# Gate and up projections of a SwiGLU layer: from a seven-product scheme (2 x 2 x 2 blocks) to a twenty-product scheme (2 width blocks, 4 contraction parts, 3 token thirds)

## The chip, the core and the metric

The kernel runs on one core of a Trainium2 chip, as one program. Its engines work side by side, each through its own queue in order: TensorE (PE, with its weight loads, PEld), VectorE (DVE), ScalarE (ACT), GpSimd (POOL) and SyncE (SP, which here only issues loads). The metric is the device time of one execution in microseconds (us), the median over several. A profile of one execution gives every instruction's start and duration.

## The reference, cut to what matters

One encoder layer over two sequences (256 and 1024 tokens, 1280 in all, width 1024): a norm, an input projection, two kinds of attention, an output projection, a residual, then

```python
h2 = rmsnorm(x, ffn_norm_g)
x = x + (jax.nn.silu(h2 @ w_gate) * (h2 @ w_up)) @ w_down
```

and a final norm. `w_gate` and `w_up` are 1024 x 2816, `w_down` is 2816 x 1024, all in float32. The change lies in `h2 @ w_gate` and `h2 @ w_up`.

## The kernel before, in words

**A product in three passes.** Every float32 operand is split into a high part (rounded to the matmul's format, by a cast on ACT) and a low part (the rest, by a subtraction). `mm3` adds three matmuls into one PSUM tile: high x high (line 110), high x low (111), low x high (112). A weight operand is "cast on ACT, low half on POOL"; a token operand is "cast on ACT, low half on DVE".

**The stage in question (M, after its PSUM tile; 791 to 1340 us of the span).** The width of 2816 is taken in eleven pairs of 128 columns (`fp`). For each pair and each of the two matrices (i = 0 gate, i = 1 up; I call one matrix of one pair a unit) the product of weights (2 width blocks x 2 contraction halves) and tokens (2 contraction halves x 2 token halves) is made by a scheme of seven products (`SEQ`), each of a sum of weight blocks with a sum of token blocks, where eight would be needed plainly. The token sums `S[m]` are made once, in and before the first pair, and kept; the weight sums are made in every unit: `sum_A` adds on POOL, `split_A` makes the two halves in a ring `wc` of six tiles. `product` runs four contraction chunks of `mm3` for each half of 640 tokens, 320 columns a time (24 matmuls), and then its result is copied (ACT, line 1050) or added (DVE, line 1052) to the unit's output `C`. Some products continue the PSUM tile of another one (`CHAIN`), so that the earlier result is read from it first.

**After a pair.** `finish` takes silu of the gate blocks (ACT, 1067), multiplies (DVE, 1069) and makes the sums that the down projection's own seven-product scheme needs (DVE, 1080); the seven results go to DRAM as `act_d[1]` to `act_d[7]`, 320 KB each, issued from ACT's queue (from POOL's in the last pair).

**What stands before.** For each of ten blocks of 128 tokens, the output projection (`out_proj`), the residual and the second norm (`ffn_in`) with transposes; the transposed block is scaled into `R` (DVE and ACT), and its token sums are begun. For blocks 0 to 4, S1 and S2 are split at once; for blocks 5 to 9 the differences are made on POOL. **What stands after** is the down projection; its first four steps are loaded and split by `down_first` inside the last pair.

**The order of work.** SP's loads stand in the order of the code. The other four engines' instructions are ordered by a scheduler at build time, which may draw an instruction ahead or put it back; `tc.issue_after(x)` keeps what it encloses behind instruction x. On the chip each engine works through its queue strictly in the order so found.

```python
def operand(A, m, ...):           # one product's weight operand
    if m == 6: ...                # s1 = A21 + A22; s2 = s1 - A11; s4 = A12 - s2 (POOL)
    if m == 7:
        sum_A(A["21"], A["11"], A["21"])
    return split_A(A[...])        # cast on ACT, subtraction on POOL
```

## Time and profile before

| | us |
|---|---|
| median of three runs (1612.8 to 1613.93) | 1613.7 |
| span of the profiled execution, first to last instruction | 1610.3 |
| what lies around the span, by difference to the median | 3.4 |
| the ten token blocks (output projection, second norm) | about 690 to 791 |
| the M stage | 791 to 1340 |
| the down projection and the end | 1340 to 1610 |

The profiled execution's own time is its span of 1610.3 us. The page gives the busy time of every engine, then groups of equal instructions: their line, engine and operation, the tiles written and read, partitions x elements, their count, total busy time and the mean of one in ns, and the idle time of the engine before them with what ended it. A matmul's duration reaches from its issue to its modelled end and overlaps the next one; the rate is the distance of starts, that is a stretch's length over its number of matmuls.

### The profile page before, as it was taken

Reading aid. Unit: us, or ns where it says so; the run is one execution under the profiler, and the core shown is the slowest. Engines: PE = TensorE matmul, PEld = TensorE weight load, DVE = VectorE, ACT = ScalarE, POOL = GpSimd, SP = SyncE. Lnnn points to the kernel's source line nnn. Section 1 sums busy time; section 2 is a strip of 40 time slices with the busy share of each in tenths; the row PEclk is TensorE's granted clock in tenths of the full one; section 3 lists DMA queues with packets and bytes.
Section 4 is the critical chain, followed back from the end, with each engine's and each line's share of the span. In section 5 each row is a group of like instructions: output and inputs, shape, how many; then the busy total and the mean of one; then the engine's idle time right before and its main releaser. Section 6 shows DMA issues by size and latency. Waiting matters only on the chain.

```text
span 1610.3 us, 25767 instructions
## 1 busy us (share of the span) xinstructions
PE 1582.5 (98%) x9616; PEld 1443.1 (90%) x9616; DVE 893.3 (55%) x1501; ACT 717.2 (45%) x1492; POOL 666.1 (41%) x833
## 2 busy tenths in 40 slices
PE   8999999999999999999999999999999999999998
PEld 8998789998888888888899999999999998888886
DVE  5853045566677777443583444334444246886676
ACT  6533144465777777544453323233222332443334
POOL 4633235544211129224676665565666651010002
PEclk9999999999999999999999999999999999999999
DMA  8626022152100030234312232222232237843534
GB/s 294 202 70 160 19 53 63 37 209 62 32 20 26 24 119 20 80 118 144 125 67 65 89 110 97 71 87 89 97 110 76 70 128 269 296 140 96 157 103 155
DMA packets 121772, 171.09 MB, mean 106 GB/s; under 512 B 35376, under 2 KB 65840, under 8 KB 121648
## 3 DMA queue, kind: packets, MB, share of 16 engines
q1 hardware_dynamic: 78880, 120.30, 24.3%
q10 hardware_dynamic: 41952, 46.08, 8.2%
q0 software_dynamic: 816, 3.08, 0.5%
q8 instruction: 75, 1.23, 0.3%
q14 instruction: 49, 0.40, 0.1%
HBM read 118.96 MB, written 50.46 MB: 105 GB/s over the span
## 4 chain that ended last, share of the span: by engine, by line
PE 90%; POOL 3%; ACT 2%; DVE 2%; DMA 1%; issue 1%; SPq 0%; ACTq 0%; POOLq 0%; DVEq 0%
PE M L112 11%; PE M L110 10%; PE M L111 10%; PE d L111 5%; PE d L110 5%; PE d L112 5%; PE o L788 4%; PE tp L778 4%; PE na_o L512 3%; PE po L110 2%; PE pj L110 2%; PE pj L111 2%; PE pj L112 2%; PE po L111 2%; PE po L112 2%; PE S L110 2%
## 5 line engine op out<-in xcount | busy, mean ns | idle before, releaser
L111 PE MATMUL M<-S,wc 128*128 128x320 f32 x1056 | 323.8, 308 | 0.0
L110 PE MATMUL M<-S,wc 128*128 128x320 f32 x1056 | 321.3, 309 | 2.5 <-ACT S L962 1.2
L112 PE MATMUL M<-S,wc 128*128 128x320 f32 x1056 | 312.0, 309 | 2.4 <-POOL wc L970 2.4
L110 PEld LDWEIGHTS M<-S,wc 128*128 128x128 f32 x1056 | 197.3, 188 | 3.7 <-ACT S L962 1.5
L111 PEld LDWEIGHTS M<-S,wc 128*128 128x128 f32 x1056 | 198.2, 188 | 0.0
L112 PEld LDWEIGHTS M<-S,wc 128*128 128x128 f32 x1056 | 194.7, 188 | 3.0 <-POOL wc L970 3.0
L970 POOL TENSOR_TENSOR wc<-A,wc 128x512 fp32r<-128x512 f32 x86 | 121.1, 1409 | 81.6 <-ACT wc L969 81.5
L1052 DVE TENSOR_TENSOR z<-M,z 128x320 f32<-128x320 f32 x120 | 57.2, 487 | 129.6 <-PE M L112 109.1
L969 ACT CAST wc<-A 128x512 fp32r<-128x512 f32 x86 | 53.5, 622 | 158.4 <-PE M L111 148.8
L970 POOL TENSOR_TENSOR wc<-sum,wc 128x512 fp32r<-128x512 f32 x62 | 88.5, 1427 | 85.8 <-ACT wc L969 85.7
L1052 DVE TENSOR_TENSOR zB<-M,zB 128x320 f32<-128x320 f32 x100 | 47.6, 488 | 133.4 <-PE M L112 109.9
L111 PE MATMUL d<-S,S 128*128 128x512 f32 (+1 forms) x314 | 121.1, 386 | 0.0
L112 PE MATMUL d<-S,S 128*128 128x512 f32 (+1 forms) x314 | 120.7, 386 | 0.0
L110 PE MATMUL d<-S,S 128*128 128x512 f32 (+1 forms) x314 | 120.4, 387 | 0.0
L100 DVE TENSOR_TENSOR PT<-tp,PT 128x512 fp32r<-128x512 f32 (+1 forms) x144 | 93.2, 658 | 33.9 <-ACT PT L99 32.7
L969 ACT CAST wc<-sum 128x512 fp32r<-128x512 f32 x62 | 38.4, 619 | 144.0 <-PE M L111 99.6
L99 ACT CAST PT<-tp 128x512 fp32r<-128x512 f32 (+1 forms) x144 | 79.2, 567 | 33.5 <-PE tp L778 30.2
L770 DVE TENSOR_REDUCE mm<-S 128x1 f32<-128x1024 f32 (+1 forms) x80 | 85.0, 1062 | 13.5 <-PE S L112 11.9
L1099 ACT CAST S<-as 128x640 fp32r<-128x640 f32 x58 | 42.2, 728 | 105.7 <-issue 62.7
L772 ACT ACTIVATE ex<-S,mm 128x1024 f32<-128x1024 f32 (+1 forms) x80 | 79.7, 997 | 14.9 <-DVE mm L770 13.6
L801 POOL TENSOR_TENSOR ob<-ob 128x128 f32<-128x128 f32 x40 | 18.5, 461 | 160.8 <-ACT ob L798 157.3
L788 PE MATMUL o<-PT,v 128*128 128x256 f32 x544 | 80.4, 287 | 0.9 <-ACT PT L99 0.9
(432 smaller groups left out, 4115.8 us busy)
## 6 DMA issues: line engine op xcount, KB each, us to landing
as<-act_d SPq DMA_DIRECT2D x73, 320.0 KB
w<-in_w_down_dram SPq DMA_DIRECT2D x44, 256.0 KB
act_d<-z ACTq DMA_DIRECT2D x35, 320.0 KB
act_d<-zB ACTq DMA_DIRECT2D x35, 320.0 KB
A<-in_w_gate_dram SPq DMA_DIRECT2D x42, 256.0 KB
A<-in_w_up_dram SPq DMA_DIRECT2D x42, 256.0 KB
x<-in_x_tm_dram SPq DMA_DIRECT2D x20, 512.0 KB
cT_d<-stg ACTq DMA_DIRECT2D x20, 320.0 KB
```

Of the source, the lines that this page charges most:

```text
L99: i = nc.scalar.copy(out=hi, in_=ps)
L100: nc.vector.tensor_sub(out=lo, in0=ps, in1=hi)
L110: nc.tensor.matmul(out, lhsT=sh, rhs=mh, start=first, stop=False, **kw)
L111: nc.tensor.matmul(out, lhsT=sh, rhs=ml, start=False, stop=False, **kw)
L112: return nc.tensor.matmul(out, lhsT=sl, rhs=mh, start=False, stop=last, **kw).ins
L770: nc.vector.reduce_max(out=nm[:, u:u + 1], in_=S, axis=AX.X, negate=True)
L772: nc.scalar.activation(ex, S, AF.Exp, bias=nm[:, u:u + 1], scale=1.0, accum_out=l[:, u:u + 1])
L778: nc.tensor.transpose(tp[:, j], ex[:, kt * P:(kt + 1) * P], ident)
L788: nc.tensor.matmul(oT, lhsT=vv, rhs=pt[s][g][:, j], start=kt == 0 and s == 0, stop=kt == nkt - 1 and s == 1)
L969: i0 = nc.scalar.copy(out=hi, in_=raw)
L970: i1 = nc.gpsimd.tensor_tensor(out=lo, in0=raw, in1=hi, op=ALU.subtract)
L1052: nc.vector.tensor_add(out=o, in0=ps, in1=a)
```

## The change

The weights of a unit are now 2 width blocks x 4 contraction parts, the tokens 4 contraction parts x 3 thirds of 428 columns (the last third has 424 tokens and four columns of zeros). The scheme has 20 products where 24 would be needed plainly, each of one width block, one contraction part (two chunks of 128) and one third: six matmuls of 128 x 128 with 128 x 428. So a unit has 120 matmuls of 428 columns where it had 168 of 320.

- **Token sums.** `X` holds the transposed tokens (4 parts x 3 thirds). Five token operands (S9, S13, S17, S3, S2) are made while the ten blocks run, hung on chosen instructions of blocks 4, 5, 7 and 8 (`LATER`); six sums are made for 296 columns after the last block. The other fifteen (`NEW_S`) are made one by one in the first pair by `build_S`: the sum's remainder of 132 columns on DVE, the cast of 856 columns on ACT, the subtraction on DVE. All of these sums stand on DVE, where before POOL had those of blocks 5 to 8.
- **The first pair** makes gate and up together: each weight operand is a tile of 2 x 256, summed and split for both matrices at once, in a ring of three slots, two products ahead.
- **The other twenty units.** `pairs` makes the 20 operands of a unit in nine steps, two operands of 256 at a time, into a ring of four slots (`wr0` to `wr3`): sums on POOL, the cast on ACT, the low half on POOL (six steps) or on DVE (three). `advance` issues a step when the slot's last product stands in the code (`LAST`). The very last unit has its operands one by one, and stops reading the gate's raw weights early, so that `down_first` can use their place.
- **Loads.** A unit's raw weights come as one load of 1 MB (before: four of 256 KB), two units ahead.
- **Results.** A product's PSUM chain (A to E) is read while other chains run, then continued: the first write of an output piece is a copy on ACT (line 1113), later ones additions on DVE (line 1111). Three `C` tiles take turns. The products of a pair's activations stand after products 10 and 15 (block "22", then "12") and after the pair's last product ("11", "21"). `act_d[3]`, `[5]`, `[1]`, `[2]` and `[6]` are stored then ("store 3" and so on in the prediction).

The core of the diff:

```diff
-    SEQ = (1, 2, 6, 7, 4, 5, 3)
-    CHAIN = {2: 1, 4: 7, 3: 5}
+    SEQ = ((1, "A", ((0, 2),)), (9, "C", ((1, 0), (1, 2))), (17, "B", ((1, 1),)),
+           (20, "A", ((1, 2),)), (13, "C", ()), (16, "B", ((1, 2),)), (14, "C", ((1, 1),)),
...
+    def build_S(n):
...
+        if n in LAST_SUMS:
+            sums(dve, slice(296, XC), *LAST_SUMS[n])
...
+        put_S(n, X[RAW[n]], n == 10)
...
+    def product(C, chains, written, seq, at, w, bank=None):
+        n, ch, out = seq[at]
+        onto = ch in chains
...
+        for kc in range(2):
+            ks = slice(kc * P, (kc + 1) * P)
+            last = mm3(ps, w[0][:, ks], w[1][:, ks], h[:, kc], l[:, kc], kc == 0 and not onto,
+                       kc == 1, onto)
+        for f, j in out:
+            o = C[:, f, j * XC:j * XC + XN[j]]
+            if (f, j) in written:
+                nc.vector.tensor_add(out=o, in0=ps[:, 0:XN[j]], in1=o)
+            else:
+                nc.scalar.copy(out=o, in_=ps[:, 0:XN[j]])
+                written.add((f, j))
...
+        def step(k):
+            if k == 0:
+                sum_w(T0, pair(5, 7), ADD, pair(6, 8))
+                sum_w(pair(6), pair(2), SUB, pair(6))
+                split(two(2), (1, 9))
+            if k == 1:
+                sum_w(T1, pair(2).unsqueeze(1).to_broadcast([P, 2, 256]), SUB, T0)
+                split(T1, (17, 20))
+            if k == 2:
+                split(pair(4, 6), ((13, 11), 14), nc.vector)
+            if k == 3:
+                split(T0, (16, 19))
...
+            if k == 6:
+                sum_w(pair(4), pair(4), ADD, pair(7))
+                sum_w(T2_[:, 1], T0[:, 0], SUB, pair(4))
+                split(T2_, (4, 10))
+            if k == 7:
+                x = raw[:, i, 0:4].rearrange("p (a b) n -> p b a n", b=2)[:, 1]
+                sum_w(T1, T1, ADD, x)
+                split(T1, (3, 2))
...
+    LAST = (1, 3, 8, 7, 11, 16, 15, 14, 19)
...
-    f["w_gate"] = a["w_gate"][0].reshape(2, 4, P, NF // 2, 2, P).transpose(3, 4, 0, 2, 1, 5)
+    f["w_gate"] = a["w_gate"][0].reshape(4, 2, P, NF // 2, 2, P).transpose(3, 2, 4, 0, 1, 5).reshape(
+        NF // 2, P, 8, 256)
```

How the order moves, at the places that the prediction speaks of. First TensorE at the start of a steady unit. Before, the first product (tile S1, weights `wc_11269`, low half `wc_11270`) starts with its high halves for both token halves, and the last product of the unit before (`zA`) is drawn in between:

```order
L110 MATMUL M1_11273<-S1_8101,wc_11269 128x320
L111 MATMUL M1_11273<-S1_8101,wc_11269 128x320
L110 MATMUL M0_11287<-S1_8101,wc_11269 128x320
L111 MATMUL M0_11287<-S1_8101,wc_11269 128x320
L110 MATMUL M1_11190<-zA_9666,wc_11224 128x320
```

After, in the unit whose tile is `C_11174`; `wr0` holds the operands of products 1 (chain A, `M0_11177`) and 9 (chain C, `M1_11185`), `wr1` that of 17 (chain B, `M0_11199`), `wr2` that of 11 (chain E, `M1_11243`); of the first rows of each product:

```order
L110 MATMUL M0_11177<-s1_9376,wr0_8113 128x428
L111 MATMUL M0_11177<-s1_9376,wr0_8113 128x428
L110 MATMUL M1_11185<-SE_8098,wr0_8113 128x428
L111 MATMUL M1_11185<-SE_8098,wr0_8113 128x428
L110 MATMUL M0_11199<-SE_8098,wr1_8114 128x428
L111 MATMUL M0_11199<-SE_8098,wr1_8114 128x428
L112 MATMUL M0_11199<-SE_8098,wr1_8114 128x428
```

After these, the rest of 17, four matmuls of 11, and only then the rest of 1 and 9 follow, so that product 1 needs its low half as the 15th matmul; 16, 20 and 13 come next, 13 as the 37th matmul (36 stand before it), then 14, 19, 12, 15, 4, 18, 3, 10, 2, 8, 7, 6 and 5. The products are thus drawn apart further than in `SEQ`.

POOL in a steady unit. Before, eleven operations of 512, sums (L980) and low halves (L970):

```order
L980 TENSOR_TENSOR sum_13512<-A21_13445,A22_13447 128x512
L980 TENSOR_TENSOR A21_13445<-A11_13441,A21_13445 128x512
L970 TENSOR_TENSOR wc_13411<-sum_13277,wc_13410 128x512
L980 TENSOR_TENSOR sum_13513<-sum_13512,A11_13441 128x512
L970 TENSOR_TENSOR wc_13450<-A11_13441,wc_13449 128x512
```

After, fifteen operations (L998 sums, L992 low halves), of which these follow each other; `wt0`, `wt1`, `wt2` are sums, `wraw` the raw weights:

```order
L992 TENSOR_TENSOR wr2_9306<-wt0_8115,wr2_9306 128x512
L998 TENSOR_TENSOR wt0_8115<-wraw_8112 128x512
L998 TENSOR_TENSOR wraw_8112<-wraw_8112 128x256
L992 TENSOR_TENSOR wr0_8113<-wt2_9308,wr0_8113 128x512
L998 TENSOR_TENSOR wt2_9308<-wraw_8112 128x512
L992 TENSOR_TENSOR wr1_8114<-wt1_9307,wr1_8114 128x512
```

The low half of products 4 and 10 (from `wt2`) waits for a slot; behind it stand a sum for the next unit and the low half of products 3 and 2 (from `wt1`). Before, a ring of six tiles held three operands; now four slots hold eight.

ACT at the end of a pair. Before, the stores of `act` (L67) stand between casts (L969), and the first copies of the next unit (L1050) among them:

```order
L67 DMA act5_d3_109<-zB_10773 128x640 [waits DMAHW1_49,DVE_49]
L67 DMA act4_d3_98<-zB_10774 128x640 [waits DVE_49]
L67 DMA act7_d3_131<-zB_10774 128x640 [waits DVE_49]
L67 DMA act1_d3_65<-zB_10773 128x640 [waits DVE_49]
L969 CAST wc_11336<-sum_11333 128x512 [waits PE_49,Activation_49,Pool_49]
L1050 COPY z_11259<-M1_11273 128x320 [waits DMAHW5_49,PE_49]
L969 CAST wc_11370<-A21_11265 128x512 [waits PE_49,Pool_49]
```

After, the copies of chains B, A and twice C (L1113) of the new unit stand between the stores of the old pair, each of which waits for its DVE operation:

```order
L990 CAST wr3_9722<-wt0_8115 128x512 [waits PE_49,Activation_49]
L1113 COPY C_10987<-M1_10990 128x428 [waits PE_49]
L67 DMA act3_d4_88<-C_10987 128x640 [waits DMAHW6_49,DVE_49]
L1113 COPY C_11174<-M0_11199 128x428 [waits DMAHW1_49,PE_49]
L1113 COPY C_11174<-M0_11177 128x424 [waits PE_49]
L67 DMA act5_d4_110<-C_10987 128x640 [waits DVE_49]
L990 CAST wr0_8113<-wt0_8115 128x512 [waits PE_49,Pool_49]
L1113 COPY C_11174<-M1_11185 128x428 [waits PE_49]
L67 DMA act1_d4_66<-C_10814 128x640 [waits DVE_49]
L1113 COPY C_11174<-M1_11185 128x424
```

Before, a unit's first copies stand behind four stores at most and its next product can run on the other PSUM tile; now two stores stand between the copies that chain C needs.

525 lines of the change are left out of this document (312 added, 213 removed), and 8 rows, old and new, of tables (SEQ, SEQ0).

## The prediction

> **What bounds the kernel now.** I read the page's first part and the chain that ended last, then TensorE's matmuls per stretch, then who waits for whom in the gate/up stage (I call it the M stage, after its PSUM tile).
>
> ```profile
> span 1610.3 us, 25767 instructions
> PE 1582.5 (98%) x9616; PEld 1443.1 (90%) x9616; DVE 893.3 (55%) x1501; ACT 717.2 (45%) x1492; POOL 666.1 (41%) x833
> PE 90%; POOL 3%; ACT 2%; DVE 2%; DMA 1%; issue 1%; SPq 0%; ACTq 0%; POOLq 0%; DVEq 0%
> ```
>
> TensorE carries 90% of the chain. A busy TensorE is not one at its peak, so matmuls have to be counted per stretch (busy time of PE, PEld, DVE, ACT, POOL with counts, clock, DMA share, GB/s):
>
> ```profile
> 690.00:790.00 100.00, 99.99 (x489) 81.00 (x489) 36.54 (x54) 39.50 (x97) 41.71 (x59) 1.00 0.37 129
> 791.20:1340.30 549.10, 544.16 (x3704) 542.45 (x3703) 258.38 (x344) 175.83 (x316) 343.62 (x246) 1.00 0.28 91
> 800.00:850.00 50.00, 45.86 (x309) 44.93 (x308) 42.39 (x45) 25.25 (x38) 39.77 (x23) 1.00 0.18 60
> 940.00:1040.00 100.00, 100.00 (x684) 100.00 (x683) 42.61 (x61) 29.11 (x53) 60.78 (x46) 1.00 0.27 89
> 1400.00:1500.00 100.00, 100.00 (x442) 82.58 (x441) 72.28 (x110) 39.73 (x68) 6.82 (x5) 1.00 0.43 131
> ```
>
> The M stage takes 549.1 us and holds 3,696 matmuls of 320 columns (the 3,704 include eight transposes). In its steady part one starts every 100/684 = 0.1462 us, with no idle time. In the down projection, 512 columns go every 100/442 = 0.2262 us.
>
> ```profile
> PE M L112 <- POOL wc L970: 2.4, 2, 2.0
> PE M L110 <- ACT S L962: 1.2, 1, 1.2
> PE M L110 <- ACT wc L969: 0.9, 1, 0.9
> PE M L110 <- DVE z L1052: 0.4, 1, 0.4
> ```
>
> These are all waits of TensorE from 780 to 1345 us: 4.9 us. So the stage is bound by matmul columns, and the other engines have room: POOL 61%, DVE 43%.
>
> **1. The matmuls: -33.5 us.** Before: 11 pairs x 2 matrices x 7 products x 4 parts x 3 x 2 halves = 3,696 of 320 columns. After: 11 x 2 x 20 x 2 x 3 = 2,640 of 428 (four columns of the last third are padding). Between the two steady rows a column costs (0.2262 - 0.1462)/192 = 0.417 ns, so 428 columns take 0.1462 + 108 x 0.417 ns = 0.191 us. 512 columns also run slower elsewhere: in the output projection
>
> ```profile
> 703.07 0.40 PE L110 MATMUL po<-wo,mT 128*128 128x512 f32 x1
> 705.40 0.40 PE L111 MATMUL po<-wo,mT 128*128 128x512 f32 x1
> ```
>
> are ten steps apart, 0.233 us each, which makes 428 columns 0.195 us. I take 0.192, near the down projection, because that stretch, like the M stage, runs nothing but three-pass products. Then 2,640 x 0.192 = 506.9 us against 3,696 x 0.1462 = 540.4. Ends: -36 (0.191) and -25 (0.195). A unit (one matrix, one pair) falls from 24.6 us to 120 x 0.192 = 23.0.
>
> The Trainium skill (TensorE: Matmul & The Clock Gate, Back-to-back issue gap) gives N/2.4 + 2.5 ns for an isolated gap, that is 135.8 ns at 320 columns, where this trace has 146.2. With its smaller fixed part, fewer matmuls save less: 502.1 - 477.4 = 24.7 us as an estimate. The trace has a fixed part of about 13 ns, and I keep that.
>
> **2. The first pair: +3.5 us.** These prices serve here and below (the last five groups from 840 to 1340 us alone):
>
> ```profile
> L96 POOL TENSOR_TENSOR w<-w_raw,w 128x256 fp32r<-128x256 f32 x4 | 2.9, 730 | 0.0
> L980 POOL TENSOR_TENSOR sum<-sum,A 128x512 f32<-128x512 f32 x20 | 25.9, 1294 | 0.7
> L980 POOL TENSOR_TENSOR sum<-A,sum 128x512 f32<-128x512 f32 x20 | 30.5, 1526 | 1.6
> L969 ACT CAST wc<-sum 128x512 fp32r<-128x512 f32 x60 | 37.1, 619 | 142.9 <-PE M L111 98.5 <-DVE zB L1052 24.7 <-DVE z L1052 19.8
> L1050 ACT COPY z<-M 128x320 f32<-128x320 f32 x40 | 16.9, 421 | 21.3 <-DVE zB L1080 11.3 <-PE M L112 10.0
> L1052 DVE TENSOR_TENSOR z<-M,z 128x320 f32<-128x320 f32 x104 | 49.4, 488 | 126.1 <-PE M L112 105.6 <-DMA A<-in_w_gate_dram 20.5
> L1080 DVE TENSOR_TENSOR z<-z 128x640 f32<-128x640 f32 x25 | 33.8, 1368 | 0.5
> ```
>
> By width, a 428-column PSUM add on DVE is 0.65 us and a copy on ACT 0.56. DVE's 640-wide SBUF operations have two prices, by what POOL does meanwhile:
>
> ```profile
> 1043.37 0.81 DVE L1069 TENSOR_TENSOR z<-z 128x640 f32<-128x640 f32 x1
> 1046.96 1.64 POOL L970 TENSOR_TENSOR wc<-sum,wc 128x512 fp32r<-128x512 f32 x1 [4.19 <-ACT wc L969]
> 1047.48 1.80 DVE L1080 TENSOR_TENSOR z<-z 128x640 f32<-128x640 f32 x1
> 1048.67 1.76 POOL L980 TENSOR_TENSOR sum<-A,sum 128x512 f32<-128x512 f32 x1
> ```
>
> (and, from the output projection, ACT's issue of one store)
>
> ```profile
> 701.67 0.33 ACTq L67 DMA_DIRECT2D xm_d<-x  x1
> ```
>
> Alone 0.81, beside POOL 1.80; POOL goes from 1.29 to 1.64-1.76. An 856-column token sum or split is then 1.08 us alone.
>
> After the last output projection, 9, 13 and 17 are ready: 6 x 1.15 = 6.9 us of matmuls, with the transposes 8.1. Product 14, the fourth, waits for the last token block in the new order: residual add, square (behind ACT's copies of product 9), rstd, scaling, transposes, scaled copies, seven 132-column sums on DVE, cast and split, about 12.5 us by these rows. Idle 4.4. Then POOL issues 27 operations of 512 (16 low halves, 11 sums) behind the last rstd, from about 4.7 us on. The eighteenth, for product 12, is due at 12.5 and seven products of 2.3, 28.6 us; at 1.3 to 1.5 each it comes at 28.1 to 31.7: late by 0 to 3, I take 3. DVE's 18 token operations and 22 PSUM adds, 19.4 + 14.3 = 34 us, fit into the pair's 46.1. Idle in all some 7.5 us, where now it is 4.1 of 50 (the row 800:850). Ends: -2, with the sums ready in time, and +12: POOL at 39.77/23 = 1.73 us, as in that row, and DVE's token operations at 1.80 widened to 2.4, which make 43 + 14.3 = 57.6 us of DVE, 11.5 more than the pair's matmuls.
>
> **3. From the first pair to the second: +3 us** (1 to 5). The first pair makes its sigmoid and nine DVE operations of 640 after its last product; the next unit's copies stand behind them on ACT. Priced as item 4, with nine operations for six.
>
> **4. The nine later pair ends: 9 x 0.8 = +7.2 us.** On ACT's queue the first copies of the new unit stand between the stores of act, each held by a DVE operation, and TensorE can't add onto chain C (product 13, matmul 36, at 6.9 us) before both copies from it. With 0.33 for a store's issue, from the pair's last matmul: cast 0.62 and copy 0.56 to 1.2; DVE at 1.8 while POOL works, to 3.05 and 4.6, then 0.81 to 5.4; store 3 lets copies B and A go by 4.6; store 5 by 5.8, cast 6.4, copy C 7.0, store 1 7.35, second copy 7.9: 1.0 late, with the copies at their proportional, upper price; I take 0.8. With DVE at 0.81 throughout, the copy ends at 6.6: 0. At 1.80 throughout it ends at 9.4: 2.5, or 22.5 us for nine.
>
> **5. Weights inside the units: 20 x 0.15 = +3 us.** POOL issues 11 operations of 512 and 4 of 256 a unit: 11 x 1.30 + 4 x 0.73 = 17.2 us of 23.0; before 11 of 512. The tightest low half (products 4 and 10, then 3 and 2) is issued when product 14 frees its slot (matmul 48, 9.4 us): cast 0.62, subtraction, sum, subtraction at 1.3 each: 13.9, due at 15.6. Covered by 1.7, which two disturbances of 0.5 don't take. Low end 0; the high end is a rival.
>
> **6. Edits with little cost.** The token sums of blocks 4 to 8 add some 15 us of DVE to its 36.5 in the row 690:790, and take POOL's differences away; TensorE's 99.99 covers them while DVE is below the stage, and if a transpose comes late: +1 (0 to 3). Loads: 1 MB once where 256 KB came four times, the same bytes; at 89 GB/s for 0.27 of the engines a full share moves 1 MB in 3.2 us, and some 13 are there between the last read and the next sum; SP has nothing else behind that wait. In the last pair nine DVE operations and seven POOL stores follow the last product, but four prefetched steps (15 matmuls each, 13.6 us) cover their loads: +1 (0 to 4).
>
> Sum: -33.5 + 3.5 + 3 + 7.2 + 3 + 2 = -14.8. The span goes from 1610.3 to 1595.5. The median, 1613.7, has 3.4 us around the profiled span; I keep these: **1599 us**.
>
> **Rivals.**
> - *POOL becomes the bound (slower).* Place: the weight operands of the 20 single units. If the SBUF operations of DVE (three splits, four or five products a unit) keep meeting POOL, its operations cost 1.9 and 1.1 and the unit 11 x 1.9 + 4 x 1.1 = 25.3 us, not 23.0: 46 us for 3, so 1642. It decides from 0.9 us a unit on, where a 512 operation averages 23.9/13.2 = 1.81. For it: 1.64 and 1.76 above; against: 1.29 to 1.53 in the groups, and PSUM adds, most of DVE's work, keep 0.488. Chance 0.15. The Trainium skill (GPSIMD Engine Reference, Key points) says that POOL shares its SBUF interfaces with VectorE and contends with operations of two SBUF inputs, which speaks against sums on both engines; the trace agrees, 0.81 against 1.80.
> - *Every pair end at 2.5 us*, the first at 5: +17.3, 1616. For it: ACT's copies already wait 11.3 us for DVE's L1080; against: POOL pauses. Chance 0.13.
> - *The first pair at its end of +12*, bound by DVE: 1607.5. For it: POOL's 1.73 in that row; against: DVE is busy there for 42 of 50 us and TensorE loses 4. Chance 0.12.
> - *The output projection's rate, 0.195 us:* -25, 1607.5. For it: the 0.233 rows; against: 0.2262 in like work. Chance 0.10. The Trainium skill's gap, above, would end at nearly the same time.
> - *Everything hidden:* items 2, 4 and 5 nothing, item 3 at 1: -30.5, 1583. Chance 0.10.
>
> The forecast as summed (1590 to 1603) has 0.40. From 1583 to 1616 lie five cases with 0.85; only the POOL case is outside: range 1582 to 1616. Two tenths of a per cent, 3.2 us, is about what a measurement tells from no change. Faster: 0.40 + 0.12 + 0.10 + 0.10 and a third of the pair ends, 0.76; the rest of these is 0.05 same and 0.04 slower, with POOL's 0.15 slower 0.19.
>
> **What would show it.** Matmul starts 0.192 us apart and a unit of 23.0 us prove item 1; 0.195 the fourth rival. Waits of TensorE for ACT's copies (L1113) right after pair ends are item 4; for POOL's low halves (L992), above all of products 3, 2, 1 and 9, the first rival, with POOL over 90% busy. An idle TensorE before product 14 and before 12, 19 and 18 is item 2. The forecast is wrong if POOL's mean for 512 passes 1.8 us, or if waits come at every unit and not at every pair.

## The result and the profile after

The changed kernel takes 1636.5 us (median of four runs, 1635.5 to 1637.4), the kernel before 1613.2 us on the same chip: a ratio of 1.014, 95% interval 1.0125 to 1.0154. It is slower by 23 us where I had forecast 1599 us, 15 us faster. The profiled execution has a span of 1635.2 us, 24.8 more than before; the sums below are made against that.

First the page's head and the chain that ended last:

```profile
span 1635.2 us, 23820 instructions
PE 1569.2 (96%) x8560; PEld 1398.4 (86%) x8560; DVE 1032.9 (63%) x1624; ACT 774.5 (47%) x1576; POOL 747.0 (46%) x922
PE 80%; DVE 11%; ACT 3%; issue 2%; DMA 2%; POOL 1%; SPq 0%; ACTq 0%; POOLq 0%; DVEq 0%
```

TensorE's share of the chain fell from 90% to 80%, and DVE has what it lost (before 2%, now 11%). Next all waits of TensorE in the M stage, 780 to 1365 us. They come to 38.9 us; before they came to 4.9. The profile counts a wait from the modelled end of the matmul before it, so between two starts somewhat more is lost:

```profile
PE M L110 <- ACT wr L990: 10.6, 11, 1.2
PE M L111 <- DVE s L959: 9.1, 1, 9.1
PE M L110 <- ACT C L1113: 8.1, 11, 1.1
PE M L110 <- DVE C L1111: 6.7, 4, 3.7
PE M L112 <- POOL wr L992: 2.4, 1, 2.4
```

The two groups of eleven waits on ACT are about one of each kind a pair; the 9.1 us are a single wait in the first pair. Then matmuls per stretch (columns as in the prediction): the first pair, one steady pair, six slices of 5 us inside the first pair, and the down projection of after and, last, of before:

```profile
794.38:864.56 70.18, 52.88 (x250) 48.26 (x248) 56.88 (x60) 34.73 (x55) 50.79 (x35) 0.88 0.10 38
916.57:965.64 49.07, 47.23 (x241) 44.92 (x240) 32.00 (x38) 18.99 (x32) 39.16 (x30) 1.00 0.25 90
805.00:810.00 5.00, 1.08 (x2) 0.50 (x2) 5.00 (x5) 2.48 (x4) 5.00 (x5) 0.59 0.00 0
810.00:815.00 5.00, 0.00 (x0) 0.00 (x0) 5.00 (x4) 0.91 (x1) 4.92 (x4) 0.50 0.00 0
815.00:820.00 5.00, 3.90 (x12) 3.67 (x13) 5.00 (x7) 0.29 (x1) 0.14 (x1) 0.54 0.00 0
820.00:825.00 5.00, 5.00 (x28) 4.84 (x27) 4.98 (x6) 2.75 (x5) 3.33 (x3) 1.00 0.01 2
840.00:845.00 5.00, 1.62 (x5) 1.54 (x6) 4.76 (x7) 2.14 (x3) 2.94 (x2) 0.85 0.00 0
845.00:850.00 5.00, 5.00 (x23) 4.78 (x22) 3.30 (x4) 1.90 (x4) 1.30 (x1) 0.81 0.00 0
1361.96:1627.53 265.57, 265.01 (x1171) 217.18 (x1169) 189.61 (x282) 105.64 (x177) 21.03 (x29) 1.00 0.53 177
1340.45:1602.96 262.51, 262.51 (x1171) 217.45 (x1170) 187.78 (x279) 104.47 (x176) 19.84 (x28) 1.00 0.53 177
```

The first pair takes 70.2 us (before 55.3). A steady pair takes 49.1, as before (49.2), with 240 matmuls for 336. Inside a steady pair a matmul starts every 0.195 us, which makes 46.8 us; 2.4 us go with the two waits (0.86 and 1.31 us between starts, and 0.1 more for the matmul after each). The slices show TensorE standing still for nine microseconds (0 matmuls from 810 to 815), DVE and POOL both full up to 815, and the granted clock at half (0.50); the next eight matmuls start 0.36 us apart. In the last two slices the same comes once more, shorter: the wait of 3.7 us for a DVE addition, and then some three microseconds of matmuls at half clock.

Here is what DVE and POOL do in that stretch (the timeline: start, duration, engine; the last bracket is idle time before and what ended it):

```profile
804.75 0.74 DVE L965 TENSOR_TENSOR st<-x,x 128x264 f32<-128x264 f32 x1
805.42 5.74 DVE L965 TENSOR_TENSOR x<-x,x 128x264 f32<-128x264 f32 x4
806.60 1.45 POOL L992 TENSOR_TENSOR wr<-wt,wr 128x512 fp32r<-128x512 f32 x1
813.80 1.34 POOL L998 TENSOR_TENSOR wr<-wt,wraw 128x512 f32<-128x512 f32 x1
813.94 2.11 DVE L959 TENSOR_TENSOR s<-st,s 128x856 fp32r<-128x856 f32 x1
815.97 0.42 DVE L965 TENSOR_TENSOR x<-x,x 128x264 f32<-128x264 f32 x1
820.41 1.48 POOL L992 TENSOR_TENSOR wr<-wraw,wr 128x512 fp32r<-128x512 f32 x1 [5.28 <-ACT wr L990]
```

A token sum of 264 elements (two chunks of 132 columns) takes 1.43 us (5.74 for four) while POOL runs one operation after the other, and 0.42 us in POOL's pause after 815.1. Product 14's low half (813.94) stands behind seven operations like these.

And ACT at the beginning of a steady pair (pair from 1063.97; L67 are stores of the old pair, L1113 copies for the new one), with the two matmuls that wait:

```profile
1065.96 0.33 ACTq L67 DMA_DIRECT2D act_d<-C  x1
1067.69 0.51 ACT L1113 COPY C<-M 128x424 f32<-128x424 f32 x1 [0.80 <-PE M L112]
1069.64 0.33 ACTq L67 DMA_DIRECT2D act_d<-C  x1
1070.07 0.62 ACT L990 CAST wr<-wt 128x512 fp32r<-128x512 f32 x1 [1.86 <-DVE C L1138]
1071.30 0.51 ACT L1113 COPY C<-M 128x424 f32<-128x424 f32 x1 [0.19 <-issue]
1071.87 0.46 PE L110 MATMUL M<-SE,wr 128*128 128x428 f32 x1 [0.72 <-ACT C L1113]
1074.95 0.62 ACT L990 CAST wr<-wraw 128x512 fp32r<-128x512 f32 x1 [3.13 <-DVE C L1138]
1075.62 0.46 PE L110 MATMUL M<-s,wr 128*128 128x428 f32 x1 [1.15 <-ACT wr L990]
```

ACT stands 1.86 us at a store that waits for DVE (L1138); the copies of chain C behind it end at 1071.8, and product 13 starts at once. Then two more stores hold ACT for 3.13 us, and product 12's weights are cast behind them.

### The profile page after: what moved, and what is told of

Read it like the earlier page. It is cut to its first block, busy times and chain, and to the rows that moved or that the text cites. A ratio compares the mean times of both kernels' runs of the same rounds, so it can differ in the third digit from the quotient of the medians.

```text
span 1635.2 us, 23820 instructions
## 1 busy us (share of the span) xinstructions
PE 1569.2 (96%) x8560; PEld 1398.4 (86%) x8560; DVE 1032.9 (63%) x1624; ACT 774.5 (47%) x1576; POOL 747.0 (46%) x922
## 4 chain that ended last, share of the span: by engine, by line
PE 80%; DVE 11%; ACT 3%; issue 2%; DMA 2%; POOL 1%; SPq 0%; ACTq 0%; POOLq 0%; DVEq 0%
PE M L110 8%; PE M L111 8%; PE M L112 8%; PE d L110 5%; PE d L112 5%; PE d L111 5%; DVE C L1138 4%; PE o L788 4%; PE tp L778 4%; PE na_o L512 3%; PE pj L110 2%; PE pj L111 2%; PE pj L112 2%; PE po L110 2%; PE po L111 2%
## 5 line engine op out<-in xcount | busy, mean ns | idle before, releaser
L1111 DVE TENSOR_TENSOR C<-M,C 128x428 f32<-128x428 f32 (+1 forms) x242 | 143.1, 597 | 148.8 <-PE M L112 78.4
L992 POOL TENSOR_TENSOR wr<-wt,wr 128x512 fp32r<-128x512 f32 (+1 forms) x112 | 154.4, 1378 | 102.3 <-ACT wr L990 102.2
L110 PE MATMUL M<-s,wr 128*128 128x428 f32 x352 | 128.5, 366 | 17.6 <-ACT wr L990 10.3
L990 ACT CAST wr<-wt 128x512 fp32r<-128x512 f32 (+1 forms) x112 | 67.4, 602 | 154.1 <-PE M L111 126.6
L111 PE MATMUL M<-s,wr 128*128 128x428 f32 x352 | 127.4, 362 | 9.1 <-DVE s L959 9.1
L112 PE MATMUL M<-s,wr 128*128 128x428 f32 x352 | 126.8, 362 | 2.4 <-POOL wr L992 2.4
L1113 ACT COPY C<-M 128x428 f32<-128x428 f32 (+1 forms) x132 | 66.3, 513 | 87.4 <-PE M L112 83.3
L990 ACT CAST wr<-wraw 128x512 fp32r<-128x512 f32 (+1 forms) x96 | 56.4, 596 | 83.0 <-PE M L111 50.5
L110 PE MATMUL M<-x,wr 128*128 128x428 f32 x264 | 94.4, 358 | 0.9 <-DVE C L1111 0.6
L112 PE MATMUL M<-x,wr 128*128 128x428 f32 x264 | 93.6, 357 | 0.0
L110 PE MATMUL d<-SE 128*128 128x512 f32 (+1 forms) x238 | 92.3, 388 | 0.6 <-DVE x L1411 0.6
L111 PE MATMUL d<-SE 128*128 128x512 f32 (+1 forms) x238 | 92.0, 387 | 0.0
L112 PE MATMUL d<-SE 128*128 128x512 f32 (+1 forms) x238 | 91.7, 387 | 0.0
L110 PE MATMUL M<-SE,wr 128*128 128x428 f32 x220 | 80.2, 365 | 9.0 <-ACT C L1113 8.1
L110 PEld LDWEIGHTS M<-s,wr 128*128 128x128 f32 x352 | 67.3, 192 | 25.0 <-ACT wr L990 13.9
L1138 DVE TENSOR_TENSOR C<-C 128x640 f32<-128x640 f32 x55 | 86.2, 1599 | 0.3
```

The costliest lines, as they stand in the source:

```text
L110: nc.tensor.matmul(out, lhsT=sh, rhs=mh, start=first, stop=False, **kw)
L111: nc.tensor.matmul(out, lhsT=sh, rhs=ml, start=False, stop=False, **kw)
L112: return nc.tensor.matmul(out, lhsT=sl, rhs=mh, start=False, stop=last, **kw).ins
L990: i0 = nc.scalar.copy(out=hi, in_=raw_)
L992: i1 = (eng or nc.gpsimd).tensor_tensor(out=lo, in0=raw_, in1=hi, op=SUB)
L1111: nc.vector.tensor_add(out=o, in0=ps[:, 0:XN[j]], in1=o)
```

## The experiments

Theories for the 24.8 us, from this profile. In the steady pairs: (S1) stores on ACT hold copies and casts, or (S2) DVE's burst of six 640-wide operations after a pair holds TensorE by itself; and the rate of 0.195 us is either the short product's or a matter of where the tiles stand. In the first pair: (F1) operations of DVE with two SBUF inputs and operations of POOL take turns, so that both together set the pair, or (F2) one engine's order does.

### The steady pairs

**stores_sp.** Stores from SP's queue (a store then waits in SP's order, behind loads):

```diff
-            (store_p if fp == NF // 2 - 1 else store)(act_d[n][fp], out)
+            (store_p if fp == NF // 2 - 1 else load)(act_d[n][fp], out)
```

> Only edit: the stores of act in pairs 0 to 9 are issued from SP's queue (behind its loads), no longer from ACT's. Theory 1, the copies of chains A, B and C stand behind stores that wait for DVE: TensorE's waits at matmuls 36 and 48 of a pair (0.86 + 1.31 us, with the slow matmul after each 2.4 us) go in pairs 1 to 10, the M stage shrinks by 20 to 24 us and the time is 1612 to 1617. Rival, DVE's burst of 640-wide operations after a pair holds TensorE by itself (through additions on chains A and C, or by the three C tiles): the wait moves from ACT's copies to DVE's additions (L1111) and less than 8 us is won, 1629 or more. Second rival, SP: the loads of raw weights now wait behind the stores and come late; waits for POOL's sums would grow and the time would rise.

1646.7 us, a miss with two causes. The first pair took 91.5 us: the loads of pair 1's raw weights stood behind the first pair's stores (the second rival). A steady pair fell to 48.25 us only.

**stores_sp2.** The same for pairs 1 to 9 (`load if fp else store`).

> As stores_sp, but the first pair's stores stay on ACT, so that SP's loads of pair 1's raw weights don't stand behind them (in stores_sp that cost the first pair 21 us). Pairs 1 to 9 store from SP. Theory from stores_sp: ACT's copies no longer hold TensorE, and of the 2.4 us of waits at a pair's beginning one of 1.4 us stays, for a DVE addition (L1111) that stands behind six 640-wide operations; a steady pair takes 48.25 us where it took 49.1, the first pair its 70.2, and the time falls by 7 to 9 us, 1627 to 1630. Rival: SP's loads come late again (each stands behind five stores of the pair before), with waits of POOL for DMA and no gain.

1628.2 us (ratio 1.0093, 1.0075 to 1.0111), as expected; all waits of TensorE from 1000 to 1280 us are now of one kind:

```profile
PE M L110 <- DVE C L1111: 7.4, 6, 1.2
```

S1 is worth 0.85 us a pair; the rest of the 2.4 us turned into a wait for DVE.

**defer, defer2.** Block 21's three operations later. In `defer` they only stood later in the code; DVE's order came out unchanged, so it tried nothing (1629.5 us, steady pair 48.25). `defer2` holds each behind an addition:

```diff
+            if late and at in (3, 5, 6):
+                with tc.issue_after(last_add[0]):
+                    next(late[0], 0)       # one operation of block 21
-            for b_ in ... ("11", "21"):
+            for b_ in ... ("11",):         # and late.append(block 21)
```

> As stores_sp2, and the three DVE operations for block 21 of a pair stand behind product 6 of SEQ in the next unit, no longer at the pair's end, so that DVE's burst of six 640-wide operations (10 us) is cut in two. Theory 1, the burst is what is left of the wait: TensorE's 1.4 us for L1111 goes as well, a steady pair takes 240 x 0.195 = 46.8 to 47.1 us, and the time is 18 to 21 us below the changed kernel's 1636.5: 1615 to 1619. Rival, DVE has no room beside POOL for these operations anywhere in the unit: the wait returns at a later product and the pair stays at 48 us or more, 1626 or more.

> As stores_sp2, and in pairs 1 to 9 the three DVE operations for block 21 are really held: each stands on DVE behind the addition (L1111) of products 20, 16 and 14 of the next unit. (In defer they stood later in the code, but DVE's order came out as before, so it tried nothing.) Theory 1, the burst of six 640-wide operations on DVE is what is left of the wait at a pair's beginning: with the additions between them TensorE's 1.4 us for L1111 goes, a steady pair falls from 48.25 to 46.8 to 47.2 us, and the time from 1628.2 to 1617 to 1620. Rival, DVE beside POOL has no room: the wait returns at a later product, 1625 or more.

`defer2`: ratio 1.0078 (1.0061 to 1.0095), that is some 1625 us and not 1617 to 1620; a steady pair takes 47.8 us. A wait of 0.9 us came back some twenty matmuls later, for an addition behind the held operations: half theory, half rival.

**spread.** On top of `combined` (below), the three held operations stand behind products 20, 19 and 15 (`at in (3, 7, 9)`), and the six of the first pair are spread in the same way.

> combined, with the three held operations of a pair (block 21) spread further: behind the additions of products 20, 19 and 15 of the next unit (they were behind 20, 16 and 14), and the first pair's six behind 9, 20, 16, 19, 15 and 12. Theory: the 0.9 us by which TensorE still waits in a steady pair of combined (at matmul 72, for an addition behind these operations on DVE) goes; a steady pair takes 46.8 to 47.0 us instead of 47.8 and the time falls by 6 to 8 us, 1615 to 1618. Rival: DVE is late by all that it has to do beside POOL in this stretch, and the wait moves to the next addition; 1621 or more.

1613.9 us, ratio to before 1.0006 (0.9996 to 1.0015). Between 1000 and 1280 us the waits of TensorE list no row at all, and a steady pair is 46.7 us:

```profile
1011.33:1058.03 46.70, 46.70 (x242) 45.06 (x241) 31.51 (x38) 18.88 (x32) 40.64 (x30) 1.00 0.26 94
```

So S1 and S2 are both true and come one behind the other: 0.85 us a pair for the stores, 1.5 for the burst. What is left in these pairs is the rate.

**columns.** Fewer columns in each steady pair; the left-out ones are missing from the result.

```diff
-            last = mm3(ps, ..., h[:, kc], l[:, kc], ...)
+            nc.tensor.matmul(ps[:, 0:cols], lhsT=..., rhs=h[:, kc, 0:cols], ...)
```

> The matmuls of pairs 1 to 10 run on fewer columns of the same tiles: 428, 424, 420, 416, 412, 408, 400, 384, 320 and 428 in pairs 1 to 9 and 10 (the first matmul of a chain and the last of each product keep 428; the columns left out are missing from the result). Looked at is the distance of starts in runs of equal matmuls. The kernel before has 146.2 ns at 320 columns and 226.5 at 512, that is 12.9 ns + 0.4167 x columns; the changed kernel has 195 at 428 where this line gives 191.2. Theory 1, the short products of two chunks have a larger fixed part of 16.7 ns: 150 ns at 320, 176.7 at 384, 190 at 416. Theory 2, something in the tiles (their place in memory, their length of 428) costs: then 146 to 147 at 320 and 173 at 384, and the excess of about 4 ns is there only for lengths that are no multiple of 16 or 32 (412, 420, 424, 428).

Median distance of starts, in ns, beside 12.9 + 0.4167 x columns, the line through 320 and 512:

```
columns   320    384    400    408    412    416    420    424    428
measured  147    175    181    186    187    189    191    193    195
line      146.2  172.9  179.6  182.9  184.6  186.2  187.9  189.6  191.2
```

The excess over the line grows, not quite evenly, from 0.8 to 3.8 ns, without a step at multiples of 16 or 32: neither theory. At 320 columns the short product is about as fast as the long one was (147 ns for 146.2), so a larger fixed part falls; from 320 to 428 columns this stage pays 48 ns over 108, some 0.44 ns a column and not 0.417.

**place.** Where operands stand in memory, at two places (448 columns from chunk to chunk in five token operands, and 16 columns further for the fourth weight tile):

```diff
-            S[n] = ls.tile([P, 2, 2, XC], ...)
+            S[n] = ls.tile([P, 2, 2, 448 if n in (14, 16, 11, 1, 20) else XC], ...)[:, :, :, 0:XC]
-        w_ring.append(rS.tile([P, 4 * XC], F32R, name="st")[:, 0:1024]
+        w_ring.append(rS.tile([P, 4 * XC], F32R, name="st")[:, 16:1040]
```

> Two edits of placement, in two stages. (a) The token operands 14, 16, 11, 1 and 20 have 448 columns from one chunk to the next, so that each chunk starts at the same place within 256 bytes as the weights of slots wr2 and wr3; the others keep 428. (b) The fourth weight tile of the down projection starts 16 columns later in st, so that it stands like the three in SE within 512 bytes. Theory 1, the matmul's rate depends on how moving and stationary operand stand in memory: matmuls of 428 columns on these five operands start 191 us/1000 apart where the others stay at 195, and the 512-column matmuls on st go from 233 to 226 ns. Rival, the place doesn't matter: 195 and 233 stay. The time changes by 0 to -3 us.

1634.5 us in one run. The five token operands stayed at 194 to 196 ns, so this shift doesn't change the rate of 428 columns. The shifted weight tile did it: rows twelve matmuls apart, first of after, then of `place`:

```profile
1389.34 0.39 PE L110 MATMUL d<-st,SE 128*128 128x512 f32 x1
1392.14 0.39 PE L110 MATMUL d<-st,SE 128*128 128x512 f32 x1
...
1388.99 0.39 PE L110 MATMUL d<-st,SE 128*128 128x512 f32 x1
1391.71 0.39 PE L110 MATMUL d<-st,SE 128*128 128x512 f32 x1
```

2.80/12 = 0.233 us against 2.72/12 = 0.227, and the down projection took 263.4 us for 265.6. The three weight tiles in SE and the activations beside them all stand at multiples of 512 bytes from SE's start; by the sizes in the code st begins 20 x 428 x 4 = 34,240 bytes behind it, 448 over a multiple, and the shift adds the missing 64. Whether the place of the moving tile counts by itself or against the stationary one, this run doesn't tell apart.

### The first pair

**hold_sums.** POOL's sums from product 16 on wait for token operand 14:

```diff
+            if at == 2:
+                with tc.issue_after(low_S[14]):
+                    nc.vector.memset(tmp[1][:, 0, 0:2], 0.0)   # the next sum of POOL writes here
```

> Only edit, in the first pair: POOL's weight sums from product 16 on wait until the low half of token operand 14 is made (a 2-element memset on DVE behind it, on which the first of these sums depends). Theory 1, DVE's token sums are slow because POOL works beside them: the seven sums of 264 elements, 1.43 to 1.5 us each in the changed kernel, fall to 0.4 to 0.45, product 14 starts 6 to 8 us earlier, TensorE's idle stretch before it shrinks from 9.1 to 1 to 3 us, and the granted clock stays near 1.0. Against that POOL starts some 5 us later than before, so products 16 and 11 can wait 1 to 4 us for their low halves (L992). Net -4 to -10 us, 1626 to 1632. Rival, the sums are slow by their own shape: they stay at 1.4 to 1.5, product 14 comes as late and POOL's delay is added, 1638 to 1645.

1637.8 us, where 1626 to 1632 were expected. DVE with POOL standing still, and then TensorE's two longest waits in the pair:

```profile
804.33 1.46 DVE L965 TENSOR_TENSOR x<-x,x 128x264 f32<-128x264 f32 x4
806.39 1.05 DVE L959 TENSOR_TENSOR s<-st,s 128x856 fp32r<-128x856 f32 x1
807.71 2.16 DVE L959 TENSOR_TENSOR s<-st,s 128x856 fp32r<-128x856 f32 x1
...
PE M L112 <- POOL wr L992: 7.2, 1, 7.2
PE M L110 <- DVE C L1114: 5.8, 3, 3.7
```

The first half of F1 is shown: a sum takes 0.43 us for 1.43, the split 1.05 for 2.11, and product 14 comes 8.3 us earlier. From 807.5 us on, with POOL at work, the next split takes 2.16 again. But POOL is now behind, and its low half for product 16 costs 7.2 us. The pair takes 72.7 us.

The Trainium skill (SBUF — State Buffer, SBUF: two separate sides) calls what these engines share an exclusive lock, held for a whole instruction, not a split of bandwidth; the trace agrees: 0.43 + 1.29 alone and 1.45 together, 1.05 + 1.29 and 2.1, 0.81 + 1.29 and 1.80, each the sum less 0.2 to 0.3.

**warm.** Forty matmuls that nobody reads, in the 9.1 us wait:

```diff
+        if at == 3:
+            for _ in range(4):
+                idle = pm[1].tile([P, 512], F32, name="M1", bufs=4)[:, 0:XC]
+                ...                          # ten matmuls of 428 columns into it
```

> Only edit, in the first pair: 40 matmuls of 428 columns on operands already there, into four PSUM tiles that nobody reads, stand on TensorE between product 17 and product 14, inside the 9.1 us wait for token operand 14 (40 x 0.195 = 7.8 us). Theory 1, the matmuls at 0.35 us apart after the wait come from the clock that the idle time lowered: the granted clock stays at 1.0 from 805 to 825 us, the matmuls of product 14 and after are 0.195 apart, and the first pair gets 2.5 to 4.5 us shorter, 1632 to 1634. Rival, the slow matmuls wait for operands (token halves that arrive late): they stay 0.35 apart and the time is the same within 1 us. If the wait is shorter than 7.8 us the rest of it is added.

1637.9 us; the first pair took 70.4 us. The windows that had 0.59, 0.50 and 0.54:

```profile
805.00:810.00 5.00, 4.78 (x24) 4.62 (x25) 5.00 (x5) 2.58 (x4) 5.00 (x5) 1.00 0.00 0
810.00:815.00 5.00, 3.50 (x18) 3.04 (x17) 5.00 (x4) 0.91 (x1) 4.92 (x4) 1.00 0.00 0
815.00:820.00 5.00, 3.65 (x11) 3.44 (x12) 5.00 (x6) 0.00 (x0) 0.38 (x1) 0.66 0.00 0
```

The clock does follow the idle time, but 3.2 us between two starts were left and they were enough: seven matmuls still came 0.36 apart. Nothing was gained in time: what follows in the pair waits for DVE anyway (4.6 us for two additions).

**no_weight_sums.** Eleven of POOL's sums of the first pair are left out (raw blocks take their place):

```diff
+            v = b(PLAIN[n]) if plain and n not in (9, 17) else value(n)
```

> Leaves out, in the first pair alone, the eleven weight sums on POOL behind product 17 (products 16, 15, 20, 18, 2, 7 and those that share their sums take raw blocks, so the first pair's numbers are not the scheme's); casts, low halves, token sums and all matmuls stay. Theory 1, DVE's operations on two SBUF inputs and POOL's take turns, so that the first pair is as long as both together (27 operations of POOL at 1.3 us and some 22 us of DVE): without 11 of them product 14 starts 6 to 8 us earlier (POOL stands still in that stretch), the waits at products 14 and 5 shrink, and the first pair falls from 70.2 to 56 to 61 us, the time to 1622 to 1628. Rival, the chain through the last token block and the ring of three weight slots sets the pair: it stays above 66 us.

1636.4 us in one run. Product 14 came 7.8 us earlier, and the pair's own matmuls ended after 60.0 us (69.5 in after), as the theory has it (56 to 61). But pair 1 gave it back: its first matmul waited 5 us for a cast (L990; the 65.1 us in the table below hold that wait), and it took 57.5 us for 52.0. The next row is why: POOL waits for the raw weights, which are loaded only when the first pair has read its own.

```profile
POOL wt L998 <- DMA wraw<-in_w_gate_dram: 5.2, 1, 5.2
```

**combined, combined_hold.** `defer2` with the first pair's stores on SP behind `load_raw(1, i)`, its blocks 11 and 21 spread over the next unit, its two silus in the other order, and the shift of `place`; then with `hold_sums` in a better order:

```diff
+            behind = normed[0] if at < 3 else lows[4] if at < 5 else lows[at]
-            with tc.issue_after(normed[0]) if at else ExitStack():
+            with tc.issue_after(behind) if at else ExitStack():
```

> defer2, and three more edits: the first pair's stores go to SP too, behind the loads of pair 1's raw weights; its operations for blocks 11 and 21 stand behind additions of the next unit one by one; the fourth weight tile of the down projection is shifted by 16 columns as in place. Theory: what the first pair's end costs pair 1 (52.0 us where a steady pair takes 49.1) is the same mechanism, stores on ACT ahead of copies and a burst of nine operations on DVE; it falls by 2 to 5 us, the down projection by 1.4 to 2.2, against defer2. With the first pair still at 70 us the time is 1611 to 1616, no better than before the change. Rival: pair 1 is held by the loads of its raw weights (issued when the first pair's last operand has read them), then it stays at 52 and the time at 1616 or more.

> combined, and in the first pair POOL's weight sums are held as in hold_sums but ordered: product 16's sum and low half first, then each product's sums behind the low half of the product two ahead. In hold_sums product 14 came 8.6 us earlier, and then TensorE waited 7.5 us for one low half on POOL that stood behind three sums that are needed later. Theory 1, that wait is an order on POOL: the first pair falls from 70.2 to 60 to 65 us and the time to 1603 to 1610, below the kernel before. Rival, POOL and DVE together are full in this pair (25 operations of POOL and 30 of DVE that take turns): waits only move, the pair stays at 68 to 71 us and the time is that of combined.

1623.4 and 1623.6 us (ratios 1.0059 and 1.0068), both misses. In `combined` pair 1 took 53.4 us and not 2 to 5 less than 52.0: the rival. In `combined_hold` the order took the 7.2 us apart into four waits for POOL, of 2.4 at most, 7.5 together: the rival again.

**spread_dve, spread_dve_hold.** Low halves from POOL to DVE: `operands_of(both, tmp, ring, (14, 11, 1, 12, 7, 8, 5, 6))` for `(14,)`, without and with the hold.

> spread, and in the first pair the low halves of eight weight operands that need no sum of their own there (14, 11, 1, 12, 7, 8, 5, 6; before, 14 alone) are made on DVE (0.68 us for 512 columns) and not on POOL (1.3). Theory 1, DVE's operations on two SBUF inputs and POOL's take turns, and the first pair lasts as long as both together: each of the seven moved operations costs 0.6 us less of that common time, and the first pair and the second become 3 to 6 us shorter together. Rival, DVE's own queue sets the first pair: seven more operations of 0.7 to 1.8 us make it 4 to 8 us longer.

> spread_dve with POOL's sums of the first pair held and ordered as in combined_hold. Theory 1: now POOL has 20 operations behind product 14 and not 27, so that the 8 us won before product 14 are not paid back in waits for its low halves; the first pair takes 58 to 64 us and the time is 1605 to 1612, below the kernel before. Rival: as in combined_hold the waits only move, and the time is within 2 us of spread_dve.

1614.7 and 1612.4 us; ratios 1.0003 (0.9992 to 1.0014) and 0.9993 (0.9984 to 1.0002). The first pair fell by 3.2 and 5.3 us against `spread`, and pair 1 grew by 3.1 and 2.7. So `spread_dve` won nothing over the two pairs together, and in `spread_dve_hold` the first pair took 66.2 us and not 58 to 64.

**adds_first, adds_first_dve, pool_pause.** Token operands behind due additions (with two more edits, as the expectation says); the same with the late low halves on DVE; and a pause for POOL.

```diff
-            with tc.issue_after(cast[0]):
+            with tc.issue_after(cast[0]), (tc.issue_after(last_add[0]) if at > 4 else ExitStack()):
                 build_S(NEW_S[at])
...
+            with tc.issue_after(first_mul[0]):                  # pool_pause
+                nc.vector.memset(tmp[2][:, 0, 0:2], 0.0)        # a sum of POOL writes here
```

> spread_dve_hold with three edits at the first two pairs: from product 20 on, each token operand of the first pair is made on DVE behind the additions of the products before it (in spread_dve_hold an addition stood behind them and TensorE waited 4.7 us for it at 838 us); the low halves of 7, 8, 5 and 6 go back to POOL; the first pair's six held operations start behind product 20 of the next unit, not behind 9. Theory: the waits for additions in the first pair (2.2 + 4.7 us) fall to 2 to 3 in all, and the 9.45 us that one 640-wide operation of DVE took beside seven operations of POOL in a row at the pair's end (it takes 0.8 alone) do not come back, since POOL pauses for ACT's casts there; together 4 to 8 us: 1604 to 1609, below the kernel before at 1613. Rival: the waits move to the casts of the token operands that now come later, 1611 or more.

> adds_first, but with the low halves of 7, 8, 5 and 6 on DVE as in spread_dve. Theory 1, POOL and DVE take turns and DVE makes a half in 0.7 where POOL needs 1.3: no slower than adds_first by more than 1 us in the first pair, but POOL's operations of the next pair come in a row and may lock out the first 640-wide operation of DVE again, as in spread_dve and spread_dve_hold (9.5 us); then pair 1 is 2 to 4 us longer than in adds_first. Rival: that long operation came from something else than POOL's run; then there is none here.

> adds_first, and at the end of the first pair one of POOL's sums for the next unit (wt2) waits for DVE's first 640-wide multiplication (through a 2-element memset behind it), so that POOL pauses once in the run of seven operations beside which that multiplication took 8.5 us (0.8 alone). Theory 1, DVE gets at its operands when POOL pauses: the multiplication takes 0.8 to 2 us, DVE is 6 to 7 us earlier in the second pair, the wait of 3.3 us for its addition there goes, against up to 2 us of POOL being later; the time falls by 1 to 4 us against adds_first, 1607 to 1610. Rival, the long operation has another cause (its own operands, the tile just written by ACT): it stays at 8 to 9 us and the time at 1611 or more.

1611.4, 1612.5 and 1612.1 us; ratios 0.9993 (0.9984 to 1.0002), 0.9999 (0.999 to 1.0007) and 0.9987 (0.9977 to 0.9996). DVE and POOL at the end of the first pair in `adds_first`, then in `pool_pause`:

```profile
859.23 10.38 DVE L1141 TENSOR_TENSOR C<-C 128x640 f32<-128x640 f32 x2 [1.00 <-ACT C L1134]
859.40 0.74 POOL L999 TENSOR_TENSOR wt<-wt 128x256 f32<-128x256 f32 x1
861.32 1.29 POOL L992 TENSOR_TENSOR wr<-wt,wr 128x512 fp32r<-128x512 f32 x1
865.79 1.29 POOL L992 TENSOR_TENSOR wr<-wt,wr 128x512 fp32r<-128x512 f32 x1
867.17 1.76 POOL L999 TENSOR_TENSOR wt<-wraw 128x512 f32<-128x512 f32 x1
...
861.92 1.28 POOL L992 TENSOR_TENSOR wr<-wraw,wr 128x512 fp32r<-128x512 f32 x1
863.16 0.83 DVE L1143 TENSOR_TENSOR C<-C 128x640 f32<-128x640 f32 x1 [2.32 <-ACT C L1134]
864.09 1.32 POOL L999 TENSOR_TENSOR wt<-wraw 128x512 f32<-128x512 f32 x1 [0.88 <-DVE wt L1233]
```

In `adds_first` a multiplication that takes 0.8 us alone lasted 8.5 (10.38 with the next one), until POOL, after a run of operations at full speed, paused for 0.1 us at 867.1. With a pause it takes 0.83. I had expected it the other way round in `adds_first` and `adds_first_dve`: it was there in the first and absent in the second. None of the three did what was expected of its time. In `adds_first` TensorE now waits 3.2 us for the cast of a token operand that comes later, which is the rival. In `pool_pause` the mechanism is the theory's, but nothing is won: that wait is 4.8 us there, the first pair takes 66.7 us for 63.8, and pair 1 53.5 for 53.8. In `adds_first_dve` that wait is 4.8 us as well, and the first pair takes 68.4 us where at most 1 more than 63.8 was expected.

The first two pairs in all these kernels (from the starts of their matmuls; the matmuls alone are 93.5 us, before 98.2):

```
                  first   second  both
before            55.3    49.9    105.2
after             70.2    52.0    122.2
hold_sums         72.7    52.1    124.8
no_weight_sums    65.1    57.5    122.6
combined          71.7    53.4    125.0
combined_hold     69.8    54.3    124.1
spread            71.6    51.4    122.9
spread_dve        68.3    54.4    122.8
spread_dve_hold   66.2    54.1    120.3
adds_first        63.8    53.8    117.6
adds_first_dve    68.4    51.3    119.7
pool_pause        66.7    53.5    120.2
```

Each row is one profile. In `stores_sp2`, `defer` and `defer2`, which leave the first pair's code as it is, it took 71.3 to 71.7 us for the 70.2 of after, so differences of 1 to 2 us say nothing.

The ten edits put the first pair between 64 and 73 us, and both together between 118 and 125. The reading is F1 in the main. That DVE and POOL lengthen each other's operations there is shown, and with eleven operations of POOL left out, some 14 us at 1.3, the pair's matmuls ended 9.5 us earlier, 7.8 of them before product 14; edits of the order mostly moved a wait. That both together leave no room in the pair is argued and not shown: in after DVE is busy for 56.9 and POOL for 50.8 of the 70.2 us, and neither alone fills it. The order has its part (F2). `adds_first`, mostly an edit of the order, is 2.7 us shorter in the two pairs than `spread_dve_hold`, but the ratios of the two are the same, 0.9993. What the pair would cost with no contention was not tried, and what sets its length is open beyond the chain to product 14.

The best version is level with the kernel before, 0.9987 at best, no more.

## Why the prediction was wrong, by its own steps

The M stage is 567.4 us for 549.1. Against the prediction's terms, in us of the profiled span (all differences of starts of matmuls; the loss of a pair is its length less its matmuls):

| term | predicted | measured |
|---|---|---|
| 1 matmuls (0.192 us) | -33.5 | 2,640 x 0.1949 = 514.5 against 540.3: -25.8 |
| 2 first pair | +3.5 | loss 23.4 against 6.1: +17.3 |
| 3 first to second pair | +3 | 5.2 against 0.8: +4.4 |
| 4, 5 nine later pairs | +7.2, +3 | pairs 2 to 9 19.1 against 1.0, the last 5.2 against 0.9: +22.4 |
| 6 the rest | +2 | loop +1.8, down projection +3.1, before and behind +1.7: +6.6 |
| sum | -14.8 | +24.9 |

**Item 1, mis-sized.** I took the down projection's rate because its work is alike. The output projection's rows gave 0.195, and that is what came: the fourth rival, 7.7 us.

**Item 2, the step that failed most.** I priced the last block's chain at 12.5 us to product 14; its low half came after 21.7. The seven 132-column sums stood in that chain at 1.43 us each beside POOL, for 0.42 alone, and the split at 2.11 for 1.05; with POOL held (`hold_sums`) the same chain takes 13.4 us. I had rows for it, 0.81 alone and 1.80 beside POOL, but used them only in the upper end, for the total of DVE's work, not for this chain. That end has a slip as well: its 11.5 us of idle time, less the 4.1 of before as in the item's own sum, would be +7.4 and not +12. The second wait that I priced, 3 us for POOL's low half of product 12, didn't come: no matmul of the first pair waits for POOL (the 2.4 us in the list lie at the start of the second). In its place came two waits for additions on DVE, 1.0 and 3.9 us between starts, and some 3.3 us of matmuls at half clock. I had no term for either.

**Item 4, right in mechanism, mis-sized.** The copies of chain C between the stores were the place (0.86 us, I had taken 0.8), but I stopped there. Behind them stood two more stores and the cast of product 12's weights (1.3 us), and behind those DVE's burst. `stores_sp2` shows that with the stores gone from ACT 1.5 of 2.4 us remain. The second rival's number came, 2.5 us at every pair end, but not its way: it had the copy of chain C 2.5 us late, and that copy was 0.86 late.

**Item 3** was in its range (1 to 5) by luck. I had priced ACT's copies behind DVE; no copy was waited for there. What came was 2.6 us for a low half of POOL, some 1.5 us at half clock and 0.7 us for an addition. **Item 5** was too dear: no steady unit waits for POOL. **The first rival** didn't come: it needed 1.81 us as the mean of POOL's operations of 512, and behind the first pair they average 1.48. The largest group in the page, with a few operations of 256 in it:

```profile
L992 POOL TENSOR_TENSOR wr<-wt,wr 128x512 fp32r<-128x512 f32 (+1 forms) x112 | 154.4, 1378 | 102.3 <-ACT wr L990 102.2
```

**Item 6.** A load of 1 MB takes 5.1 us from issue to first use (849.2 to 854.35 in `no_weight_sums`), where I had estimated 3.2; in steady units it stays hidden. In the down projection I had no term for the fourth weight tile, which `place` prices at 1.5 us by its matmuls (222 x 6.6 ns) and 2.2 by the stage; the other 0.7 are not explained. Of the 1.7 us before and behind, 1.4 lie ahead of the token blocks, where the code is the same: the output projection began anywhere from 659.8 to 661.5 us in the profiles of these kernels (659.9 before, so the blocks don't start at about 690, as I had put it). The loop's 1.8 us are inside the 0 to 3 that I gave a late transpose. They go with two waits of its transposes' matmuls for DVE that the kernel before doesn't have, which I read from the profile and didn't try:

```profile
PE trm L893 <- DVE mT L100: 1.3, 2, 0.8
```

**The range** failed for a reason of its own: what three rivals cost came in the same execution, the rate by its own mechanism, the pair ends and the first pair by others. I had priced each alone, as an alternative (1616, 1607.5, 1607.5). They lie in different places, so their prices add: -14.8 + 17.3 + 8.5 + 8.5 = +19.5, or 1633. The range held each of them alone; the pair ends with either of the others left it.

My two signs of a wrong forecast, POOL's mean above 1.8 us and waits at every unit, didn't appear either. Of the signs that I gave for the terms and the fourth rival three did: 0.195 us between starts, waits for L1113 at the steady pair ends, and an idle TensorE before product 14.

## What to carry to other kernels

A matmul count saves only what the stage's other engines leave room for: here 5% fewer matmul-microseconds came with 44 us of new losses in the stage, and removing the steady ones took three edits one behind the other, because each wait hid the next. Price a sum or a split on DVE at its time beside POOL wherever it stands in a chain that TensorE waits for. Keep stores that wait for a late result off a queue whose next instruction TensorE needs, and put loads ahead of them on the queue that takes them.

## What the runs showed of the hardware that I had not expected

- A short DVE operation with two SBUF inputs costs about 1 us more beside POOL, where an operation of POOL takes 1.29: 264 elements 0.42 us alone and 1.43 beside it, 640 elements 0.81 and 1.80. And DVE may not get its turn between two operations of POOL that follow at once: one multiplication lasted 8.5 us beside seven of them (9.5 in `spread_dve_hold`, 9.6 in `spread_dve` and `combined_hold`); in `adds_first_dve` it did get in. What decides is open; in `adds_first` it ended when POOL paused, and with the pause of `pool_pause` it didn't come.
- TensorE's granted clock was 0.50 three times in the M stage of the changed kernel: from 805.9 to 819.6, from 843.5 to 846.9 and from 870.8 to 874.2 us, once for 13.7 and twice for 3.4 us. Matmuls then start 0.36 us apart. No matmul had started for 2.3 us before the first stretch (and for 9.7 inside it), for 4.1 before the second, and for 2.8 shortly before the third, where matmuls had run again for 1.2 us. The 3.2 us left in `warm` were enough too; 2.9 us in `stores_sp2` and in `no_weight_sums` were not. The Trainium skill (TensorE: Matmul & The Clock Gate, Part 1: The HAM clock gate) gives a window of about 3.4 us that runs freely and halves the clock when it was idle; by it 428 columns need 357 ns, an estimate. The trace agrees with 0.36 us and with stretches of 3.4 us; but here less than a whole window without matmuls was enough.
- A 512-column matmul took 233 ns or 227 by where its moving tile stood; for 428 columns no such effect was found, and why they take 195 ns and not 191 is open.
